# Attention's sums of later key blocks: added by VectorE before one product with the matrix of -1

## Chip, core and metric

The kernel runs on one core of a Trainium2 chip. The metric is the time of one execution on the device in microseconds (us); the number for a kernel is the median of its runs. The engines are called PE (TensorE), DVE (VectorE), ACT (ScalarE), POOL (GpSimd) and SP (SyncE, which issues the transfers here).

## What is computed

A trunk of two layers on 512 tokens of width 1024, in float32. Each layer is a SwiGLU feed-forward half, a token mixer and a second SwiGLU half, each between two RMSNorms. The change is in the mixer's attention: 8 heads of 64, strictly causal, with stick-breaking weights in place of a softmax. In the reference:

```python
z = jnp.einsum('bhqd,bhkd->bhqk', q_blk, kh).astype(jnp.float32) * scale
mask = k_pos[None, :] < q_pos[:, None]
log_keep = jnp.where(mask, jax.nn.log_sigmoid(-z), 0.0)
between = lax.cumsum(log_keep, axis=3, reverse=True) - log_keep
a = jnp.where(mask, jnp.exp(jax.nn.log_sigmoid(z) + between), 0.0)
return jnp.einsum('bhqk,bhkd->bhqd', a.astype(vh.dtype), vh)
```

Since log_sigmoid(-z) is -softplus(z), and log_sigmoid(z) is z - softplus(z), the exponent of a key is its z less the softplus of that key and of all later keys up to the query.

## The kernel before

Every matrix product is made of float32 values split in a high and a low part (the function `to_parts`, lines 507 to 513: a cast makes the high part, VectorE subtracts it from the value for the low part), so that TensorE multiplies several pairs of parts where plain arithmetic would have one product. Weights come from memory in units, one per tile `raw`, and are split by ScalarE (line 155, `wh`) and VectorE (line 156, `wl`). Weights and kept activations share a pool of `SLOTS` slots. The functions `load`, `split` and `ahead` (lines 140 to 172) keep a ledger of it: a unit is loaded if a slot is free beyond the reserved ones, and split if two are.

Attention works with keys on partitions and queries on columns, in key blocks of 128. A head (class `Head`) has three tiles in PSUM: tile 0 holds key block 2 (queries 256 to 511, its columns 0 to 255) and key block 3 (queries 384 to 511, columns 256 to 383), tile 1 holds key block 1 (queries 128 to 511, 384 columns), tile 2 key block 0 (512 columns).

`scores` computes z for each tile with the mask added on the diagonal blocks. Then ScalarE makes ln(1 + exp(-|z|)) in three instructions (lines 542 and 297), VectorE adds max(z, 0) (line 545), and `parts` splits the softplus: VectorE casts the high part pH (line 510) and subtracts for the low part pL (line 513).

`sums` then subtracts softplus values from z on TensorE, accumulating in the same PSUM tile. Within a key block this is a product with `ntri`, a triangle of -1. For the key blocks after it, it is a product with `none_`, a diagonal matrix of -1, which moves a softplus block of another tile onto these columns. Tile 1 needs the blocks 2 and 3 of tile 0, tile 2 needs those of tiles 1 and 0. Each such move is done for the high and for the low part. ScalarE then takes the exponential (line 297), which is split again (ScalarE casts at line 512, VectorE subtracts at line 513), and `values` multiplies it by v.

The instructions of TensorE stand in one fixed order (`mm` makes each follow the one before). Attention is a generator that the main line of the mixer's other projections polls between its products. After a head's scores come about 9.5 us of other products (`D_SUMS`, of which `values` of the previous head takes its share) and then its sums. The order on the other engines is the planner's: it takes what is ready, by program order. The softplus and attention parts of all heads take turns in `PB` pairs of buffers, other work tiles in `TB` = 7 buffers named t. Other work of VectorE during attention is splitting weights (line 156), the short convolution and the pooling (lines 664 to 701), queries and keys (lines 643 and 649), and the head's output (lines 590 and 513).

Of the kernel before, what the change touches and what calls it, by code (L numbers as in the profile page):

```python
# [12 lines left out]
ALU = mybir.AluOpType  # L13
PSUM = bass.MemoryType.PSUM

P = 128
T = 512
# [12 lines left out]
EPS = 1e-6  # L30
UNIT = KB * P
HEAD = 3
SLOTS = 28
RAW = 2
WARM = 24
URGENT = 0
# [1 line left out]
OUT_A = ((4, 6), (7,))  # L38
OUT_B = ((5, 0), (1, 2), (3,))
TB = 7  # L40
PB = 4
CB = 5

MASKED = -1e30
H_DVE = ('p0', 'p1', 'p2')

D_SUMS = 9.5
D_SCORES = 0.8
# [53 lines left out]
def trunk_kernel(ctx: ExitStack, tc: tile.TileContext, xt: bass.AP, wu: bass.AP,  # L102
                 consts: bass.AP, mats: bass.AP, gains: bass.AP, out: bass.AP):
    nc = tc.nc
# [10 lines left out]
    def uid(s):  # L115
        cnt[0] += 1
        return f"{s}_{cnt[0]}"
# [3 lines left out]

    slots = {"free": SLOTS, "reserve": CHUNKS[0]}

    def slot(name, dt=F32R):
        assert slots["free"] > 0, name
        slots["free"] -= 1
        return wpool.tile([P, 2, T], dt, tag="w", bufs=SLOTS, name=name)

# [71 lines left out]
    def tmp(shape=(P, T), dt=F32, tag="t", bufs=TB):  # L200
        return apool.tile(list(shape), dt, tag=tag, bufs=bufs, name=uid(tag))

    def bank(tag="d"):
        return ppool.tile([P, 512], F32, tag=tag, bufs=5 if tag == "z" else 3, name=uid("ps" + tag))
# [18 lines left out]
    def mm(dst, w, r, start, stop, us=None):  # L223
        ins = nc.tensor.matmul(dst, w, r, start=start, stop=stop, skip_group_check=True)  # L224
        if line["last"] is not None:
            after(ins, line["last"], "order")
        line["last"] = ins
        line["now"] += max(0.108, r.shape[-1] * 0.00042) if us is None else us
# [66 lines left out]
    def fn(out_, in_, f_, **kw):  # L295

        ins = nc.scalar.activation(out_, in_, f_, **kw)  # L297
        if last_load:
            after(ins, last_load[0], "activation table")
        last_fn[:] = [ins]  # L300
# [206 lines left out]
    def to_parts(dstH, dstL, src, what=None):  # L507

        if what in H_DVE:
            nc.vector.tensor_copy(dstH, src)  # L510
        else:
            nc.scalar.copy(dstH, src)  # L512
        nc.vector.tensor_tensor(dstL, src, f32(dstH), op=ALU.subtract)  # L513
# [5 lines left out]
    class Head:  # L519
# [6 lines left out]

        def scores(self):
            k, lh, q = (self.qk[n][:, self.e, :] for n in ("k", "lh", "q"))
            for ti, blocks in enumerate(TILES):
                z = bank("z")  # L530
                self.z.append(z)

                d, m = self.diagonals(z, blocks)
                mm(d, identr, m, True, True, 0.06 * len(blocks))
                for kb, col in blocks:
                    ks, qs = slice(kb * P, (kb + 1) * P), slice(kb * P, T)

                    for qq in (q, lh):
                        mm(z[:, col:col + T - kb * P], k[:, ks], qq[:, qs], False, True)
                n = WIDTH[ti]  # L540
                t = tmp()
                nc.scalar.activation(t[:, :n], z[:, :n], AF.Abs)  # L542
                fn(t[:, :n], t[:, :n], AF.Exp, scale=-1.0)
                fn(t[:, :n], t[:, :n], AF.Ln, bias=1.0)
                nc.vector.scalar_tensor_tensor(t[:, :n], z[:, :n], 0.0, t[:, :n],
                                               op0=ALU.max, op1=ALU.add)
                self.sp.append(self.parts(t, n, f"p{ti}"))

        def diagonals(self, t, blocks):

            n = len(blocks)
            d = t.rearrange("p (a b) -> p a b", b=P)[:, 0:2 * n - 1:2, :]
            return d, maskr.unsqueeze(1).to_broadcast((P, n, P))

        def parts(self, t, n, what):
            hi = tmp(dt=F32R, tag="pH", bufs=PB)
            lo = tmp(dt=F32R, tag="pL", bufs=PB)
            to_parts(hi[:, :n], lo[:, :n], t[:, :n], what)
            return hi, lo

        def sums(self):

            for ti, blocks in enumerate(TILES):
                z, n = self.z[ti], WIDTH[ti]
                for part in self.sp[ti]:
                    mm(z[:, :n], ntri, part[:, :n], False, True)

                for to, src, c0, w in (((P, 0, 256, P),), ((P, 0, 0, 256), (256, 0, 256, P)),
                                       ((P, 1, 0, 384), (256, 0, 0, 256), (384, 0, 256, P)))[ti]:
                    for part in self.sp[src]:  # L570
                        mm(z[:, to:to + w], none_, part[:, c0:c0 + w], False, True)
                t = tmp()
                fn(t[:, :n], z[:, :n], AF.Exp)
                self.a.append(self.parts(t, n, f"a{ti}"))
# [338 lines left out]
```

## Time and profile before

| what | value |
|---|---|
| time, median of 3 runs | 1927.26 us (1927.14 to 1928.81) |
| the profiled execution | 1925.21 us |
| its span, first to last instruction | 1923.4 us |
| instructions | 22094 |
| mean granted clock of TensorE | 0.992 of full speed |
| bytes read from memory, written | 176.65 MB, 2.10 MB |

All rows are of the one profiled execution, and their times count from the start of its span. In the page, each engine has its busy time, its share of the span and its count of instructions. A row of the timeline has the start, the duration (both us), engine, line, operation and tiles, and in brackets the idle time of the engine before it and who ended that. A row of the windows has the stretch and its length, then for PE, PEld (weight loads), DVE, ACT and POOL the busy time and the count of instructions, and then the granted clock of TensorE (1.00 is full speed), the share of the transfer engines and GB/s. A row of groups has line, engine, operation, tiles, shape and count, then busy us and mean ns of one, then the idle time before.

### The profile page before, as it was taken

To read this page: it belongs to the slowest core of one execution; us is meant where nothing else is said; L and a number is where in the kernel's file an instruction comes from. 1 tells how busy PE (TensorE), PEld (TensorE's weight loads), DVE (VectorE), ACT (ScalarE), POOL (GpSimd) and SP (SyncE) were. 2 spreads that over 40 slices of the span, in tenths; PEclk is the share of its full clock that TensorE was granted. 3 is DMA by queue.
4 is the path that set the end of the run, shared out by engine and by line. 5 is a ranking of instruction groups with operands and counts; after the bars stand their busy time and mean duration, and the time that the engine had idled before them with its cause. 6 is when DMAs were issued, how large, how long until landed. Compare 5 with 4: busy or idle time off the path is not lost.

```text
span 1923.4 us, 22094 instructions
## 1 busy us (share of the span) xinstructions
PE 1883.7 (98%) x9072; PEld 1587.3 (83%) x9072; DVE 876.2 (46%) x1154; ACT 719.7 (37%) x1137; POOL 47.6 (2%) x68
## 2 busy tenths in 40 slices
PE   7999999999999999999999999999999999999998
PEld 5888888888878988888898888888888788888887
DVE  5323333567767422333463223336577663223333
ACT  4323222357764323222242222224477542322221
POOL 1000000000001000000010000000000010000000
PEclk8999999999999999999999999999999999999999
DMA  5213233131023223223142222422111242222311
GB/s 207 99 67 131 77 111 108 44 131 55 34 75 144 88 77 120 77 99 121 55 143 88 99 87 88 142 77 99 66 55 44 88 140 91 99 88 88 132 66 44
DMA packets 50645, 180.17 MB, mean 94 GB/s; under 512 B 5744, under 2 KB 5872, under 8 KB 50544
## 3 DMA queue, kind: packets, MB, share of 16 engines
q1 hardware_dynamic: 50544, 178.76, 27.0%
q8 instruction: 71, 1.16, 0.2%
q14 instruction: 30, 0.25, 0.0%
HBM read 176.65 MB, written 2.10 MB: 93 GB/s over the span
## 4 chain that ended last, share of the span: by engine, by line
PE 91%; DVE 4%; ACT 2%; issue 1%; DMA 1%; POOL 0%; SPq 0%; DVEq 0%; POOLq 0%; ACTq 0%
PE psz L224 80%; PE psd L224 11%; DVE wl L156 1%; PE psd L266 1%; DVE f L322 0%; DMA raw<-in_w_dram 0%; ACT t L297 0%; DVE f L362 0%; DVE hl L335 0%; DMA g<-in_gains_dram 0%; DVE x L376 0%; DVE pL L513 0%; POOL ss L313 0%; ACT pH L512 0%; ACT t L542 0%
## 5 line engine op out<-in xcount | busy, mean ns | idle before, releaser
L224 PE MATMUL psz<-hl,wh 128*128 128x512 f32 (+1 forms) x1536 | 566.3, 369 | 6.4 <-DVE hl L335 6.4
L224 PE MATMUL psz<-hh,wh 128*128 128x512 f32 (+1 forms) x1536 | 566.7, 369 | 4.3 <-ACT hh L334 4.3
L224 PE MATMUL psz<-hh,wl 128*128 128x512 f32 (+1 forms) x1536 | 565.5, 368 | 0.0
L156 DVE TENSOR_TENSOR wl<-raw,wh 128x1024 fp32r<-128x1024 f32 x324 | 387.0, 1211 | 313.4 <-ACT wh L155 244.2
L224 PE MATMUL psz<-wh,hid 128*128 128x512 f32 x1408 | 437.1, 390 | 0.0
L155 ACT CAST wh<-raw 128x1024 fp32r<-128x1024 f32 x324 | 328.5, 1038 | 223.4 <-PE psz L224 180.3
L224 PEld LDWEIGHTS psz<-hl,wh 128*128 128x128 f32 x1536 | 291.8, 190 | 54.6 <-DVE hl L335 7.4
L224 PEld LDWEIGHTS psz<-hh,wh 128*128 128x128 f32 x1536 | 291.7, 190 | 52.6 <-ACT hh L334 5.3
L224 PEld LDWEIGHTS psz<-hh,wl 128*128 128x128 f32 x1536 | 291.7, 190 | 47.4
L224 PEld LDWEIGHTS psz<-wh,hid 128*128 128x128 f32 x1408 | 264.3, 188 | 54.7
L224 PE MATMUL psz<-wl,hid 128*128 128x512 f32 x704 | 273.9, 389 | 0.0
L448 DVE TENSOR_TENSOR t<-t,psz 128x512 f32<-128x512 f32 x84 | 57.7, 687 | 470.3 <-PE psz L224 470.3
L449 ACT CAST hid<-t 128x512 fp32r<-128x512 f32 x88 | 54.6, 620 | 450.4 <-DVE t L448 450.4
L297 ACT ACTIVATE t<-psz 128x512 f32<-128x512 f32 (+1 forms) x136 | 77.5, 573 | 227.5 <-PE psz L224 226.6
L224 PEld LDWEIGHTS psz<-wl,hid 128*128 128x128 f32 x704 | 132.2, 188 | 27.2
L224 PE MATMUL psd<-hh,wh 128*128 128x512 f32 (+1 forms) x320 | 119.7, 374 | 0.0
L224 PE MATMUL psd<-hh,wl 128*128 128x512 f32 (+1 forms) x320 | 118.0, 369 | 0.0
L224 PE MATMUL psd<-hl,wh 128*128 128x512 f32 (+1 forms) x320 | 118.0, 369 | 0.0
L450 DVE TENSOR_TENSOR hid<-t,hid 128x512 fp32r<-128x512 f32 x88 | 61.0, 693 | 60.8 <-ACT hid L449 60.8
L313 POOL TENSOR_TENSOR ss<-ss,expo 128x1 f32<-128x1 f32 x48 | 39.1, 815 | 1689.7 <-DVE ss L372 1586.1
L224 PEld LDWEIGHTS psd<-hh,wl 128*128 128x128 f32 x320 | 60.3, 189 | 10.3
L224 PEld LDWEIGHTS psd<-hl,wh 128*128 128x128 f32 x320 | 60.4, 189 | 10.1 <-issue 0.5
(98 smaller groups left out, 1437.4 us busy)
## 6 DMA issues: line engine op xcount, KB each, us to landing
raw<-in_w_dram SPq DMA_DIRECT2D x316, 512.0 KB, 3.3
g<-in_gains_dram SPq DMA_DIRECT2D x12, 512.0 KB, 5.0
x<-in_xt_dram SPq DMA_DIRECT2D x4, 512.0 KB, 8.7
raw<-in_w_dram SPq DMA_DIRECT2D x8, 256.0 KB, 2.7
out_dram<-x SPq DMA_DIRECT2D x8, 256.0 KB, 2.1
mat<-in_mats_dram SPq DMA_DIRECT2D x1, 384.0 KB, 9.4
mat<-in_mats_dram SPq DMA_DIRECT2D x1, 64.0 KB, 3.2
cst<-in_consts_dram SPq DMA_DIRECT2D x1, 25.0 KB, 9.2
```

The lines of the kernel that those rows point to most:

```text
L155: nc.scalar.copy(h[:, :n], raw[:, :n])
L156: nc.vector.tensor_tensor(lo[:, :n], raw[:, :n], f32(h[:, :n]), op=ALU.subtract)
L224: ins = nc.tensor.matmul(dst, w, r, start=start, stop=stop, skip_group_check=True)
L266: ins = nc.tensor.transpose(dst, src, ident)
L297: ins = nc.scalar.activation(out_, in_, f_, **kw)
L313: nc.gpsimd.tensor_tensor(r, ms, expo, op=ALU.pow)
L448: nc.vector.tensor_tensor(u, g, pu, op=ALU.mult)
L449: nc.scalar.copy(t[:, 0, :], u)
L450: nc.vector.tensor_tensor(t[:, 1, :], u, f32(t[:, 0, :]), op=ALU.subtract)
```

## The change

Three additions on VectorE, as soon as tile 1's softplus is there, make one tile s of 512 columns: its columns 256 to 511 hold, for the queries 256 to 511, the softplus of blocks 2 and 3 added together, and its columns 0 to 255 hold that plus the softplus of block 1 for the same queries. This tile is split in parts once, with the high part cast by VectorE (`'later'` in `H_DVE`). The sums of tile 1 then move 256 columns of it with `none_`, and those of tile 2 move 256 columns of it, and 128 of tile 1's own. The part buffers grow from four pairs to five, and a slot is taken from the pool of weights.

```diff
-SLOTS = 28
+SLOTS = 27
-PB = 4
+PB = 5
-H_DVE = ('p0', 'p1', 'p2')
+H_DVE = ('p0', 'p1', 'p2', 'later')
...
         def scores(self):
             k, lh, q = (self.qk[n][:, self.e, :] for n in ("k", "lh", "q"))
+            ts = []
             for ti, blocks in enumerate(TILES):
...
                 self.sp.append(self.parts(t, n, f"p{ti}"))
+                ts.append(t)
+                if ti == 1:
+
+                    s = tmp()
+                    nc.vector.tensor_copy(s[:, 256:384], ts[0][:, :P])
+                    nc.vector.tensor_tensor(s[:, 384:], ts[0][:, P:256], ts[0][:, 256:384], op=ALU.add)
+                    nc.vector.tensor_tensor(s[:, :256], s[:, 256:], t[:, P:384], op=ALU.add)
+                    self.later = self.parts(s, T, "later")
...
-                for to, src, c0, w in (((P, 0, 256, P),), ((P, 0, 0, 256), (256, 0, 256, P)),
-                                       ((P, 1, 0, 384), (256, 0, 0, 256), (384, 0, 256, P)))[ti]:
-                    for part in self.sp[src]:
+                for to, src, c0, w in (((P, self.sp[0], 256, P),), ((P, self.later, 256, 256),),
+                                       ((P, self.sp[1], 0, P), (256, self.later, 0, 256)))[ti]:
+                    for part in src:
                         mm(z[:, to:to + w], none_, part[:, c0:c0 + w], False, True)
```

## Rows read from the trace of the kernel before

**Rows 1.** The page, busy time of each engine.

```profile
PE 1883.7 (98%) x9072; PEld 1587.3 (83%) x9072; DVE 876.2 (46%) x1154; ACT 719.7 (37%) x1137; POOL 47.6 (2%) x68
```

**Rows 2.** Waits of TensorE: us in total, times, longest us.

```profile
PE psz L224 <- DVE pL L513: 6.0, 10, 1.1
```

**Rows 3.** Windows: heads 0 and 1 of layer 0, then two stretches after head 6.

```profile
434.29:442.88 8.59, 8.59 (x44) 7.34 (x43) 6.97 (x14) 2.76 (x6) 0.00 (x0) 1.00 0.19 61
447.79:454.56 6.77, 6.77 (x37) 5.94 (x36) 6.73 (x13) 5.26 (x9) 0.00 (x0) 1.00 0.08 32
...
545.00:548.40 3.40, 3.40 (x16) 3.40 (x16) 2.31 (x5) 1.71 (x5) 0.00 (x0) 0.50 0.05 17
1493.00:1496.40 3.40, 3.40 (x23) 3.10 (x23) 2.98 (x5) 2.68 (x7) 0.00 (x0) 1.00 0.03 10
```

**Rows 4.** Timeline of VectorE: last pL of heads 0, 1, 4, 5, 7.

```profile
437.95 0.69 DVE L513 TENSOR_TENSOR pL<-t,pH 128x512 fp32r<-128x512 f32 x1
...
451.47 1.15 DVE L513 TENSOR_TENSOR pL<-t,pH 128x384 fp32r<-128x384 f32 x2
...
506.86 0.69 DVE L513 TENSOR_TENSOR pL<-t,pH 128x512 fp32r<-128x512 f32 x1
...
517.56 0.69 DVE L513 TENSOR_TENSOR pL<-t,pH 128x512 fp32r<-128x512 f32 x1
...
555.76 1.15 DVE L513 TENSOR_TENSOR pL<-t,pH 128x384 fp32r<-128x384 f32 x2
```

**Rows 5.** Timeline of TensorE: ntri by pL, heads 2 to 7.

```profile
472.64 0.45 PE L224 MATMUL psz<-pL,ntri 128*128 128x384 f32 x1 [0.27 <-DVE pL L513]
...
485.95 0.44 PE L224 MATMUL psz<-pL,ntri 128*128 128x384 f32 x1 [0.69 <-DVE pL L513]
...
508.39 0.39 PE L224 MATMUL psz<-pL,ntri 128*128 128x512 f32 x1
...
520.08 0.39 PE L224 MATMUL psz<-pL,ntri 128*128 128x512 f32 x1
...
542.61 0.45 PE L224 MATMUL psz<-pL,ntri 128*128 128x384 f32 x1 [1.10 <-DVE pL L513]
...
544.47 0.50 PE L224 MATMUL psz<-pL,ntri 128*128 128x512 f32 x1 [0.73 <-DVE pL L513]
...
557.86 0.39 PE L224 MATMUL psz<-pL,ntri 128*128 128x512 f32 x1
```

**Rows 6.** Timeline of TensorE, products with the matrix of -1, tile 2.

```profile
473.85 0.34 PE L224 MATMUL psz<-pH,none__73 128*128 128x384 f32 x1
474.02 0.34 PE L224 MATMUL psz<-pL,none__73 128*128 128x384 f32 x1
...
474.43 0.22 PE L224 MATMUL psz<-pH,none__73 128*128 128x128 f32 x1
474.49 0.27 PE L224 MATMUL psz<-pL,none__73 128*128 128x128 f32 x1
```

**Rows 7.** Groups by shape on VectorE: busy us, mean ns, idle before.

```profile
L513 DVE TENSOR_TENSOR pL<-t,pH 128x384 fp32r<-128x384 f32 x64 | 34.9, 553 | 6.3 <-ACT pH L512 6.0
...
L513 DVE TENSOR_TENSOR pL<-t,pH 128x512 fp32r<-128x512 f32 x32 | 22.0, 688 | 11.0 <-ACT pH L512 10.6
...
L510 DVE CAST pH<-t 128x512 fp32r<-128x512 f32 x16 | 6.7, 418 | 0.0
...
L823 DVE CAST ntri<-mat 128x128 fp32r<-128x128 f32 x1 | 0.2, 224 | 0.0
```

**Rows 8.** Groups on VectorE within head 6's window, 534.83 to 544.47.

```profile
L156 DVE TENSOR_TENSOR wl<-raw,wh 128x1024 fp32r<-128x1024 f32 (+1 forms) x3 | 3.1, 1043 | 0.0
```

**Rows 9.** Timeline: splits of the last value weights, then TensorE's first use.

```profile
388.01 1.22 DVE L156 TENSOR_TENSOR wl<-raw,wh 128x1024 fp32r<-128x1024 f32 x1
...
390.88 1.22 DVE L156 TENSOR_TENSOR wl<-raw,wh 128x1024 fp32r<-128x1024 f32 x1
...
396.27 0.39 PE L224 MATMUL psz<-wh,hh 128*128 128x512 f32 x1
```

## The prediction

> **What bounds the kernel now.** I read the page's busy shares first: TensorE (PE) is busy nearly all of the span, VectorE (DVE) less than half of it [rows 1]. So time taken off TensorE is time off the span, wherever it stays fed. The list of what TensorE waits for comes next: the waits inside the program's attention are waits for pL, the low part that VectorE writes [rows 2]. They are 6.0 us in ten pieces, which is small, but they say that in places VectorE is already the engine that sets the end of attention's sums.
>
> That is why VectorE's 46% must not be read as room. It is a mean over the feed-forward layers, where VectorE idles, and attention. So I read the windows that matter: one for each head, from VectorE's first softplus instruction (line 545) to the moment when TensorE starts the last product of that head that needs a softplus (ntri by pL, 512 columns). Head 0's window of 8.59 us leaves VectorE 1.62 idle, head 1's of 6.77 only 0.04 [rows 3]. From head 1 on it is full exactly where the change puts work.
>
> Full is not late, since some of what VectorE does in a window is not urgent (weights split for later, convolution, pooling). Lateness is read from the end of the head's last pL on VectorE against the start of its product on TensorE [rows 4, 5]: head 1, 451.47 + 1.15 = 452.62 against 454.56, the end of its window [rows 3], 1.94 us to spare; head 4, 507.55 against 508.39, 0.84; head 5, 518.25 against 520.08, 1.83; head 7, 556.91 against 557.86, 0.95. Head 0, with no head before it, ends at 437.95 + 0.69 = 438.64 against 442.88, the end of its window: 4.24, more than the change can take. Heads 2, 3 and 6 have less than nothing: TensorE stands 0.27, 0.69 and 1.10 + 0.73 us for them [rows 5]. These are 2.8 of the 3.0 us that [rows 2] leave for a layer; layer 1 repeats layer 0.
>
> **What goes, part by part.** Counted from the code, for each head and each of the two parts (high, low), the matrix of -1 multiplied 128 columns for tile 0, 256 + 128 for tile 1, 384 + 256 + 128 for tile 2. After the change it is 128, 256, 128 + 256. So one product of 384 and one of 128 columns go, twice: 4 of 12 matmuls. What they cost is the distance between starts, not the duration, because matmuls overlap: a 384 takes 474.02 - 473.85 = 0.17 us, a 128 takes 474.49 - 474.43 = 0.06 us [rows 6]. Per head 2 x (0.17 + 0.06) = 0.46 us; 16 heads: 7.4 us, 0.38% of the time. This is the most that the removal itself can give.
>
> Each of these matmuls also loads the matrix of -1 anew, and the start distance of 0.06 us shows that the load is hidden. [...]
>
> **What comes.** Five VectorE instructions a head: a copy of 128 columns, an add of 128, an add of 256, then the split of the 512 columns into a cast and a subtraction. The last two are on show: 0.42 and 0.69 us [rows 7]. An add of two SBUF operands goes by the subtraction's rows: (688 - 553) / 128 = 1.05 ns a column, so 0.28 us for 128 and 0.42 for 256. A float copy of 128 columns isn't in the trace; the cast of 128 took 224 ns, the bounds are nothing and the 0.28 of an add, I take 0.22. Sum 2.03 us of durations. Neighbours in VectorE's queue overlap by about 0.1 us where independent, so what they displace lies between 1.6 and 2.0; I take 1.9. Over 16 heads that is 30 us more for an engine with 1047 us idle overall, and nearly none idle in these windows.
>
> **When it is due.** TensorE comes to the end of the sums sooner, by the two lost 128s of tile 1, 0.1 us. And the sum's low part is needed before tile 2's, about half a microsecond earlier than the instant against which I measured (one product of the sum's 256 columns and the 512-column ntri product of the high part stand between). So each head must find 1.9 + 0.3 = 2.2 us (1.7 at least, 2.6 at most). If VectorE keeps its order and puts off nothing, the new stall of a head is 2.2 less its spare time: heads 0 to 7: 0, 0.3, 2.2, 2.2, 1.4, 0.4, 2.2, 1.3 = 10.0 us a layer, 20 in both. The same sum with 1.7 and 2.6 gives 6.7 and 12.6 a layer.
>
> Against it: VectorE's order isn't fixed by hand; the planner places what is ready, by program order. The five instructions stand in the program ahead of the weight splits and the pooling that fill the same windows, so some of this will go behind them, and splitting weights later costs nothing where they lie ready early. But it can't all go: the chain copy, add, add, cast, subtraction is serial, and in the gaps between its links a ready split of about 1 us slips in, as three do in head 6's window today, 3.1 us [rows 8].
>
> **The remaining edits.** One weight slot less (28 to 27) moves some splits one place later in the ledger of slots. The tightest place that I found is the last weight of the value projection in a mixer: its split starts 2.9 us after the one before it (390.88, 388.01) and ends at 392.10; TensorE first needs it at 396.27 [rows 9]. One place later it would end at about 395.0: hidden, with 1.3 us left. I charge nothing; a second place would cost 2.9 - 1.3 = 1.6 us a mixer. A fifth pair of part buffers is there because a head now makes seven pairs for six. The second tile's pair no longer has to wait for the previous head's values, the sum's does instead. At best this ring also ends the present waits, at worst it changes nothing; I charge nothing. The longer life of tile 0's t costs nothing as long as 7 buffers serve 8 uses a head; no row shows a wait for t.
>
> **The rivals.** *All is put off* (other sign): VectorE moves enough pooling and weight splitting behind the chain that no stall is added. In head 6's window there are 3.1 us of splits alone [rows 8], more than its 2.2. Then the full 7.4 us is kept: 1919.9. It decides if less than 3.7 us a layer of new stalls remains. *Nothing is put off*: 20 - 7.4 = +12.6, 1939.9; bounds 6.7 and 12.6 a layer give 1933.3 to 1945.1. *The ring helps*: besides the full saving the 6.0 us of waits in [rows 2] go: -13.4, 1913.9. *Weights come late*: +1.6 a mixer or more on top of half the stalls, 1934. *The clock.* After head 6's stalls in layer 0, the granted clock was 0.50 from 545.0 to 548.4, and TensorE began 16 matmuls in the time in which layer 1, after the same stalls, began 23 at 1.00 [rows 3]: half of 3.4 us lost, 1.7 us, sometimes. More stalls mean more such stretches; I charge one. [...]
>
> **How the numbers follow.** Likeliest: half of the 20 us is put off. Then -7.4 + 10.0 + 1.7 = +4.3 against the profiled execution's 1925.2, which is itself 2.0 below the median of the runs; against the median the 1.7 may be there already in part, so I take +3.7: 1931 us. Chances: half put off 0.33 (nearly as often within 0.2% as above it, seldom below), all put off 0.28 (nearly always faster), nothing put off 0.25, weights late 0.08, ring helps 0.06. A difference of 0.2% (3.9 us) is about what a measurement of this kernel can tell from no change. Faster: 0.25 + 0.06 + 0.03 = 0.34; slower: 0.25 + 0.13 + 0.03 = 0.41; the same: 0.25. Range: from all of the saving, 1919.5, to nothing put off at its middle price, 1940; the ring and the dear half of "nothing" are left out. The likeliest case's own range is 1927 to 1935.
>
> **What would show it.** 64 matmuls with the matrix of -1 a layer instead of 96, at the same start distances: if not, the first step is wrong. TensorE's waits for what VectorE writes at lines 510 and 513: some 10 us more than the 6.0 of [rows 2] is the forecast; about 6.0 again is "all put off", 26 is "nothing". If the weight splits of line 156 and the pooling's instructions have left the head windows, VectorE reordered. New waits of TensorE on wl would be the slot. A clock of 0.5 at 471 to 490 or 540 to 550 would be stalls charged twice. I'm wrong if new stalls are under 3.7 us a layer or lie elsewhere.

## The result: slower by 1.07%, and where the time went

| what | before | after |
|---|---|---|
| time, median | 1927.20 us (4 runs) | 1946.56 us (4 runs, 1945.43 to 1947.10) |
| ratio, with its 95% interval | | 1.0107 (1.0095 to 1.0118) |
| span of the profiled execution | 1923.4 us | 1944.6 us |
| mean granted clock of TensorE | 0.992 | 0.986 |

The forecast was 1931 us, the range 1919.5 to 1940: slower was the likeliest sign, but the size lies outside.

The profile after is read in the order of the prediction. First the page's busy times, which answer to [rows 1]:

```profile
PE 1888.2 (97%) x9008; PEld 1586.9 (82%) x9008; DVE 901.2 (46%) x1234; ACT 725.2 (37%) x1137; POOL 55.7 (3%) x68
```

64 matmuls are gone and 80 instructions of VectorE have come, as counted. VectorE's share is still 46%: the number that had to be distrusted has not moved. VectorE's busy time rose by 901.2 - 876.2 = 25.0 us, 1.56 a head. What TensorE waits for is the list that answers to [rows 2]:

```profile
PE psz L224 <- DVE pL L513: 20.4, 18, 2.2
PE psd L266 <- DVE f L325: 10.3, 2, 7.7
PE psd L266 <- DVE ss L372: 7.5, 3, 2.8
PE psz L224 <- DVE hl L335: 6.6, 3, 2.6
PE psz L224 <- ACT pH L512: 1.6, 2, 0.8
PE psz L224 <- DVE pH L510: 1.2, 2, 0.6
...
```

In the kernel before, these rows stand beside the one of [rows 2]:

```profile
PE psd L266 <- DVE f L325: 11.1, 4, 8.3
PE psz L224 <- DVE hl L335: 6.4, 4, 2.6
...
PE psz L224 <- ACT hh L334: 4.3, 2, 2.4
...
PE psz L224 <- DVE pH L510: 0.9, 2, 0.5
...
```

The waits for what VectorE writes at lines 510 and 513 were 0.9 + 6.0 = 6.9 us and are 1.2 + 20.4 = 21.6. A wait by way of line 372, at layer boundaries, is new, and the one on line 334 is gone. The whole list sums to 32.9 us before and 49.3 after: 16.4 us more of an idle TensorE.

The rest is clock. These windows answer to the last two of [rows 3]: two stretches that follow long waits, one after that, and one in layer 1 (columns as before; the third column from the right is the granted clock; read in windows of 0.1 us over the whole span it is 1.00 in 18908 of 19445 and 0.50 in 520, and between them in 17, at the changes):

```profile
492.20:495.60 3.40, 3.40 (x11) 2.80 (x10) 2.44 (x6) 2.58 (x5) 0.00 (x0) 0.50 0.47 151
...
553.60:560.40 6.80, 5.86 (x20) 5.15 (x20) 3.61 (x8) 4.03 (x10) 0.00 (x0) 0.50 0.02 4
560.50:567.30 6.80, 6.80 (x34) 5.71 (x33) 6.80 (x15) 4.00 (x7) 0.00 (x0) 1.00 0.00 1
1447.90:1454.70 6.80, 6.22 (x17) 5.07 (x18) 5.03 (x8) 4.91 (x8) 0.00 (x0) 0.50 0.23 78
```

In 6.8 us at 0.50 TensorE begins 20 matmuls (0.94 us of it is a wait), in the next 6.8 us 34. Over the span, (1 - 0.986) x 1944.6 = 27.2 us of clock are lost, against (1 - 0.992) x 1923.4 = 15.4: 11.8 us more, uncertain by some 2 us because the clock is given to three digits. Now the account of the two profiled executions closes: -7.4 for the products, +16.4 of waits, +11.8 of clock are +20.8 us; the spans differ by 21.2. TensorE's busy time agrees: it rose by 1888.2 - 1883.7 = 4.5 us, where -7.4 + 11.8 is 4.4.

By place, the stretches at half clock inside attention explain it. In the kernel before there is one, of 3.4 us (after head 6 of layer 0, [rows 3]). In the changed kernel there are five: 3.4 us after head 3 and 6.8 us at head 6 in layer 0, then 6.8, 3.4 and 6.8 us at heads 3, 4 and 6 in layer 1. That is 27.2 us for 3.4, so 13.6 us lost for 1.7. None follows heads 1, 2 and 5, with waits of 0.7 to 1.2 us each, nor head 4 of layer 0, which waits as long (1.55 us) as head 4 of layer 1 (1.56). Outside of attention, the layer boundaries lose 3.4 us both before (one stretch of 6.8 us at 606) and after (two of 3.4 us, at 400 and 1356).

Head 6 shows how a wait comes about. VectorE's timeline, from the third of the new instructions (line 555) to the sum's low part, with the starts that count:

```profile
545.49 0.42 DVE L555 TENSOR_TENSOR t<-t,t 128x256 f32<-128x256 f32 x1
...
547.35 0.41 DVE L510 CAST pH<-t 128x512 fp32r<-128x512 f32 x1
547.68 1.21 DVE L156 TENSOR_TENSOR wl<-raw,wh 128x1024 fp32r<-128x1024 f32 x1
548.82 0.74 DVE L678 SCALAR_TENSOR_TENSOR c<-c,cst,c 128x511 f32<-128x511 f32 x1
549.48 0.68 DVE L546 SCALAR_TENSOR_TENSOR t<-psz,t 128x512 f32<-128x512 f32 x1
550.19 0.69 DVE L599 TENSOR_TENSOR t<-psz,t 64x512 f32<-64x512 f32 x1
550.91 0.69 DVE L156 TENSOR_TENSOR wl<-raw,wh 128x512 fp32r<-128x512 f32 x1
551.52 0.68 DVE L513 TENSOR_TENSOR pL<-t,pH 128x512 fp32r<-128x512 f32 x1
```

And TensorE's, in the same stretch, which answers to the rows of head 6 in [rows 5]:

```profile
549.21 0.22 PE L224 MATMUL psz<-pH,none__73 128*128 128x128 f32 x1
549.27 0.28 PE L224 MATMUL psz<-pL,none__73 128*128 128x128 f32 x1
549.38 0.39 PE L224 MATMUL psz<-pH,ntri 128*128 128x384 f32 x1
...
552.26 0.38 PE L224 MATMUL psz<-pL,none__73 128*128 128x256 f32 x1 [2.20 <-DVE pL L513]
553.26 0.51 PE L224 MATMUL psz<-pH,ntri 128*128 128x512 f32 x1 [0.61 <-DVE pH L510]
554.70 0.80 PE L224 MATMUL psz<-pL,ntri 128*128 128x512 f32 x1 [0.94 <-DVE pL L513]
```

The sum is there at 545.9 and its high part at 547.8, but its low part comes at 552.2: weight splits, a step of the convolution, tile 2's own softplus (line 546) and an earlier head's output stand between. TensorE waits 2.20, 0.61 and 0.94 us, 3.75 in all where it was 1.83, and at 553.6 the clock falls. The window of [rows 8] has grown from 9.64 to 12.09 us (542.61 to 554.70). It holds two weight splits, of 1024 and of 512 columns, where [rows 8] has three; but the third of those starts at 544.33, 0.14 us before the window's end, so that only two stood ahead of the sums in the kernel before as well. In this head no split was put off behind them.

### The profile page after: what moved, and what is told of

Its sections match the earlier page's. It is cut to its first block, busy times and chain, and to the rows that moved or that the text cites. A ratio compares the mean times of both kernels' runs of the same rounds, so it can differ in the third digit from the quotient of the medians.

```text
span 1944.6 us, 22070 instructions
## 1 busy us (share of the span) xinstructions
PE 1888.2 (97%) x9008; PEld 1586.9 (82%) x9008; DVE 901.2 (46%) x1234; ACT 725.2 (37%) x1137; POOL 55.7 (3%) x68
## 4 chain that ended last, share of the span: by engine, by line
PE 85%; DVE 9%; ACT 3%; issue 2%; POOL 1%; DMA 1%; SPq 0%; DVEq 0%; POOLq 0%; ACTq 0%
PE psz L224 76%; PE psd L224 8%; DVE wl L156 1%; DVE pL L513 1%; ACT t L297 1%; POOL ss L313 1%; DVE t L546 1%; DVE pH L510 1%; DMA raw<-in_w_dram 1%; PE psd L266 1%; DVE f L322 1%; DVE f L362 1%; DVE x L376 1%; ACT t L543 0%; DVE t L599 0%
## 5 line engine op out<-in xcount | busy, mean ns | idle before, releaser
L224 PEld LDWEIGHTS psz<-wl,hid 128*128 128x128 f32 x704 | 132.3, 188 | 27.2
L313 POOL TENSOR_TENSOR ss<-ss,expo 128x1 f32<-128x1 f32 x48 | 47.0, 978 | 1681.6 <-DVE ss L372 1570.4
L513 DVE TENSOR_TENSOR pL<-t,pH 128x384 fp32r<-128x384 f32 (+1 forms) x112 | 66.8, 608 | 21.2 <-ACT pH L512 18.7
L224 PEld LDWEIGHTS psd<-hh,wh 128*128 128x128 f32 x320 | 62.2, 194 | 10.6 <-PE psd L224 0.5
```

What stands on the lines that cost most here:

```text
L313: nc.gpsimd.tensor_tensor(r, ms, expo, op=ALU.pow)
```

## The experiments

The waits below are those of TensorE for the pL and pH that VectorE writes at lines 510 and 513, from each run's own profile. Each ratio is to the kernel before on the same chip, whose medians there were 1926.15 us (e1 to e4), 1925.02 (e5 to e8) and 1924.81 (e9 to e12).

| run | slots, pairs, D_SUMS | ratio (95% interval) | median us | waits us | clock |
|---|---|---|---|---|---|
| before | 28, 4, 9.5 | 1 | | 6.9 | 0.992 |
| after | 27, 5, 9.5 | 1.0107 (1.0095 to 1.0118) | 1946.56 | 21.6 | 0.986 |
| e1_slot | 27, 4, 9.5 | 1.0012 (1.0003 to 1.0021) | 1928.35 | 6.8 | 0.992 |
| e2_ring | 27, 5, 9.5 | 1.0011 (1.0002 to 1.0020) | 1927.85 | 6.8 | 0.992 |
| e3_cut | 28, 4, 9.5 | 0.9977 (0.9968 to 0.9986) | 1920.52 | 8.0 | 0.991 |
| e4_four | 28, 4, 9.5 | 1.0118 (1.0105 to 1.0132) | 1948.72 | 23.8 | 0.984 |
| e5_last | 27, 5, 9.5 | 1.0139 (1.0124 to 1.0154) | 1951.89 | 26.3 | 0.984 |
| e6_own | 27, 4, 9.5 | 1.0122 (1.0105 to 1.0139) | 1948.25 | 21.2 | 0.986 |
| e7_late | 27, 5, 12.5 | 0.9976 (0.9967 to 0.9986) | 1920.65 | 4.3 | 0.991 |
| e8_cost | 27, 5, 9.5 | 1.0135 (1.0120 to 1.0150) | 1950.34 | 19.3 | 0.986 |
| e9_before_late | 28, 4, 12.5 | 0.9956 (0.9944 to 0.9969) | 1917.83 | 0.4 | 0.993 |
| e10_late_28 | 28, 4, 12.5 | 0.9927 (0.9915 to 0.9939) | 1910.70 | 4.2 | 0.993 |
| e11_narrow | 28, 4, 12.5 | 0.9930 (0.9917 to 0.9944) | 1910.75 | 1.7 | 0.993 |
| e12_mid | 27, 5, 11.0 | 1.0044 (1.0031 to 1.0056) | 1933.14 | 11.9 | 0.986 |

**e1_slot: the lost slot alone.** The kernel before with:

```diff
-SLOTS = 28
+SLOTS = 27
```

> The kernel before with one weight slot less (27 for 28) and nothing else. Theory 1 (the slot makes the new waits at the layer boundaries, the additions make those in attention): TensorE gets the three waits on VectorE line 372 that the changed kernel shows at 399, 989 and 1355 us (2.3, 2.8 and 2.4 us), saves about 3.7 us of its waits at 606 and 1552, and has one or two more stretches at half clock, 1.7 us each; in all +2 to +6 us, 1929 to 1933; its waits on pL in attention stay near 6. Theory 2 (the waits at the boundaries too come from the planner's order around the new instructions): within 2 us of the kernel before, no wait on line 372.

Measured: +0.12%, 2.2 us by the medians. The three waits by way of line 372 are there (7.1 us, against none before), and in return the wait on line 334 (4.3 us) is gone and that on line 325 is 9.2 us for 11.1. So the boundary waits belong to the slot, as theory 1 says, though they cost less than the 1929 to 1933 us expected.

**e2_ring: slot and ring of buffers, without the arithmetic.** In addition to e1_slot:

```diff
-PB = 4
+PB = 5
```

> The kernel before with 27 slots and five pairs of part buffers, without the additions: all of the change but its arithmetic. Theory 1: the same time as with the slot alone, within 2 us, and waits on pL in attention of 4 to 7 us. Theory 3 (the ring of buffers changes VectorE's order, and that makes the new waits in attention): the waits on pL rise towards 20 us, and the time to 1940 and more.

Measured: the same as e1_slot, with waits in attention unchanged at 6.8 us. Theory 3 falls for this order of the work: the ring by itself changes nothing.

**e3_cut: the saving alone.** The kernel before with:

```diff
-                for to, src, c0, w in (((P, 0, 256, P),), ((P, 0, 0, 256), (256, 0, 256, P)),
-                                       ((P, 1, 0, 384), (256, 0, 0, 256), (384, 0, 256, P)))[ti]:
+                for to, src, c0, w in (((P, 0, 256, P),), ((P, 0, 0, 256),),
+                                       ((P, 1, 0, P), (256, 0, 0, 256)))[ti]:
```

> The kernel before with the four matmuls of a head cut and no additions on VectorE; left out are the softplus sums of the blocks beyond the nearest ones. It measures the saving by itself. Theory 1: 7.4 us less on TensorE, waits as before (6 to 7 us), so 1919.5 to 1921. Theory 4 (TensorE only comes sooner to waits that end at the same time, since VectorE's chain sets them): waits on pL rise by about 1 us or more and the gain is 5 us or less.

Measured: -0.23% (-0.14 to -0.32), 4.4 us by the ratio and 5.6 by the medians. It is a gain, but less than 7.4: the waits on lines 510 and 513 rose from 6.9 to 8.0 us, and all the waits together from 32.9 to 34.9. About a quarter of what TensorE saves here it spends waiting, as theory 4 has it, though the median alone would also fit theory 1.

**e4_four: the change without the lost slot and without the fifth pair.** The changed kernel with `SLOTS = 28` and `PB = 4`.

> The changed kernel with 28 slots and four pairs of part buffers for its seven pairs a head. Theory 1: no wait on line 372 at the boundaries, the waits in attention stay near 20 us, time about 1938 to 1942. Theory 3: with four pairs the sum's and the next two pairs must wait for the values of the head before, the waits in attention rise to 25 us or more, and the time is 1945 or more.

Measured: 1.0118, no better than the change (the intervals overlap). The waits by way of line 372 are gone, but attention's are 23.8 us and the clock is 0.984. Giving the slot back does not make the change fast, which agrees with the 0.12% of e1_slot. Of the two expectations neither is met in full: the time is theory 3's, the waits lie between. Two edits were made at once, so what four pairs cost here may hide what the slot gives.

**e5_last: the same instructions, in another place.** The additions and the split of their sum stand after the loop over the tiles:

```diff
-                if ti == 1:
-                    s = tmp()
...
-                    self.later = self.parts(s, T, "later")
+            s = tmp()
...
+            self.later = self.parts(s, T, "later")
```

> The changed kernel with the three additions and the split of their sum written behind tile 2's softplus in the program instead of before it; the same instructions. Theory A (VectorE simply has 2 us more to do before the sums end): the waits on lines 510 and 513 stay within 3 us of the 21.6 of the changed kernel, time within 3 us of 1946.6. Theory B (the place of the new tile delays tile 2: in the changed kernel ScalarE's first instruction on tile 2 comes after four others of the softplus instead of after one fewer tile's worth, and its pair is made last): ScalarE takes tile 2 early again as before, the waits fall to 15 us or less, time 1940 or less.

Measured: 1.0139, waits 26.3 us. ScalarE does take tile 2 early again (its first instruction on head 6's tile 2 starts 1.30 us after that on tile 0, against 2.55 in the changed kernel), but the waits did not fall; now the sum's low part is what comes last. Theory B falls: the order decides which part is late, not whether one is. Theory A's bounds are passed too, by 1.7 us of waits and 2.3 us of time: this order is the worse one.

**e6_own: the sum outside of the ring of t.**

```diff
-PB = 5
+PB = 4
...
-                    s = tmp()
+                    s = tmp(tag="s", bufs=2)
```

> The changed kernel with the sum in two buffers of its own instead of the seven of the tiles t, paid for by the fifth pair of part buffers (four pairs, as in the run with four pairs and 28 slots; here 27). Theory A: waits in attention as in that run, 22 to 26 us, time 1948 to 1951. Theory B, if it is the turn in the ring of t that holds tile 2 back: ScalarE takes tile 2 early, waits 17 us or less, time 1943 or less.

Measured: 1.0122 and 21.2 us of waits, just under theory A's 22 to 26, and far from theory B's 17. ScalarE does take tile 2 early here (at head 6, 1.31 us after tile 0, as in the kernel before; e4_four, which has four pairs too, has 2.55), so the turn of the t buffers does hold tile 2 back in the changed kernel; but it is not the cause of the waits.

**e7_late: the same work, given 3 us more.** The changed kernel with:

```diff
-D_SUMS = 9.5
+D_SUMS = 12.5
```

> The changed kernel with 12.5 us in place of 9.5 of other products between a head's scores and its sums, so that VectorE has 3 us more; same work. Theory A and B both: nearly all waits in attention end before TensorE comes, 5 us or less remain, the half-clock stretches in attention go, and 14 us of waits and 10 us of clock come back: 1920 to 1926, unless the last head then has too little other work behind it (then waits of up to 3 us a layer at the end of attention, 1926 to 1932). Rival (TensorE's fixed order is not the point; VectorE falls behind for good and carries its delay from head to head): waits of 15 us and more stay.

Measured: 0.9976, waits 4.3 us, and no stretch at half clock in attention (mean clock 0.991 for 0.986). The same instructions now run 1.3% faster than in the changed kernel, and faster than the kernel before. This speaks for lateness: VectorE does all of the added work, and the loss is gone when TensorE comes later. (The planner orders VectorE anew for each kernel, so that an effect of its order is not wholly excluded.) What is left against the control with the same number (e9_before_late) is 0.2%, and e10_late_28 takes that back. VectorE does not carry a delay from head to head, so the rival falls.

**e8_cost: the additions without the saving.** The changed kernel with the loop of the sums of before:

```diff
-                for to, src, c0, w in (((P, self.sp[0], 256, P),), ((P, self.later, 256, 256),),
-                                       ((P, self.sp[1], 0, P), (256, self.later, 0, 256)))[ti]:
-                    for part in src:
+                for to, src, c0, w in (((P, 0, 256, P),), ((P, 0, 0, 256), (256, 0, 256, P)),
+                                       ((P, 1, 0, 384), (256, 0, 0, 256), (384, 0, 256, P)))[ti]:
+                    for part in self.sp[src]:
```

> The changed kernel with its additions and the split of the sum, but with the twelve products of before on TensorE; the sum is computed and not used. It measures the cost alone, by the side of the run that cut the matmuls alone. If cost and saving add up: 1946.6 + 5.6 to 7.4 = 1952 to 1954. If waiting for the sum itself is what costs (TensorE does not need it here): waits in attention 12 us or less and time 1940 or less.

Measured: 1.0135, waits 19.3 us. Cost and saving very nearly add up: 1.35% - 0.23% is 1.12%, and the change has 1.07%. TensorE needn't even wait for the sum: VectorE's own lateness with the softplus parts makes nearly all of it.

**e9_before_late: the control.** The kernel before with `D_SUMS = 12.5`.

> The kernel before with 12.5 us for 9.5 between scores and sums: the control for the run of the changed kernel with 12.5. Theory A: its waits on lines 510 and 513 (6.9 us) go and with them a half-clock stretch, so -3 to -9 us, 1917 to 1923, and the changed kernel's gain over this one is then only what is left of the saved products. Rival (12.5 costs something by itself, at the end of attention or by heads that take longer to start): no gain or a loss, 1925 to 1930.

Measured: 0.9956, waits 0.4 us. The kernel before was late in its own sums as well, and more time alone is worth 7 us to it. Of the gain of e7_late this much is not the change's: at the same 12.5 us the change with 27 slots and five pairs is some 0.2% slower, with intervals that just overlap, and not faster.

**e10_late_28: the change with time, and with the slot.** The changed kernel with `D_SUMS = 12.5`, `SLOTS = 28`, `PB = 4`.

> The changed kernel with 12.5, and with 28 slots and four pairs of part buffers. Theory A, and the slot's price of 2 us: waits of 5 to 8 us in attention, no waits on line 372, 1916 to 1921, some 2 us under the run with 12.5 and 27 slots. Rival (with four pairs and later sums the head's pairs wait for each other): 1922 or more, waits above 10 us.

Measured: 0.9927 (0.9915 to 0.9939), 1910.70 us: faster than both kernels, and than the control, whose interval does not touch this one. It is also less than the 1916 to 1921 expected. By the medians it is 7.1 us under the control. The profiled executions show less, 1912.3 - 1908.6 = 3.7 us, and tell why, in the control first and then here:

```profile
PE 1880.5 (98%) x9072; PEld 1586.2 (83%) x9072; DVE 876.8 (46%) x1154; ACT 717.7 (38%) x1137; POOL 47.6 (2%) x68
```

```profile
PE 1872.8 (98%) x9008; PEld 1577.4 (83%) x9008; DVE 900.0 (47%) x1234; ACT 719.6 (38%) x1137; POOL 47.6 (2%) x68
```

At the same clock, 0.993, TensorE is busy 7.7 us less: this is what the removed products are worth. Its waits are 28.9 us against 24.9, of which 4.2 against 0.4 are on lines 510 and 513, and take 4.0 of it back. The rest of the 7.1 goes with the clock: two of the control's five runs have 0.993 (1913.6 and 1914.1 us) and three 0.990 to 0.991 (1917.8 to 1919.0), and the median is one of the latter; all five of this kernel have 0.993. Why the control's clock falls more often is open. This kernel is also 9.9 us under e7_late by the medians, far more than the slot's 2.2 in e1_slot. The profiled spans differ by 12.3 us, of which the waits account for 36.1 - 28.9 = 7.2 (the waits by way of line 372 among them, 7.8 us against none), and TensorE's busy time, at a clock of 0.991 against 0.993, for 5.0. Whether the slot or the fifth pair does this was not tried apart.

**e11_narrow: less work where nothing is late.** As e10_late_28, with no copy and a sum of 384 columns; tile 1's product with 256 columns of the sum becomes two with 128:

```diff
-                    nc.vector.tensor_copy(s[:, 256:384], ts[0][:, :P])
-                    nc.vector.tensor_tensor(s[:, 384:], ts[0][:, P:256], ts[0][:, 256:384], op=ALU.add)
-                    nc.vector.tensor_tensor(s[:, :256], s[:, 256:], t[:, P:384], op=ALU.add)
-                    self.later = self.parts(s, T, "later")
+                    nc.vector.tensor_tensor(s[:, 256:384], ts[0][:, P:256], ts[0][:, 256:384], op=ALU.add)
+                    nc.vector.tensor_tensor(s[:, :P], ts[0][:, :P], t[:, P:256], op=ALU.add)
+                    nc.vector.tensor_tensor(s[:, P:256], s[:, 256:384], t[:, 256:384], op=ALU.add)
+                    self.later = self.parts(s, 384, "later")
...
-                for to, src, c0, w in (((P, self.sp[0], 256, P),), ((P, self.later, 256, 256),),
+                for to, src, c0, w in (((P, self.sp[0], 256, P),), ((P, self.sp[0], 0, P), (256, self.later, 256, P)),
```

> As the run before this one, with a sum of 384 columns for 512: the copy is gone, tile 1 takes blocks 2 from its own parts, and VectorE has about 0.35 us less a head. Theory A: little is left to gain where TensorE comes late, so within 2 us of it, waits at most 2 us fewer. If VectorE's work still sets the end: 3 us or more less.

Measured: 0.9930, the same as e10_late_28, with waits of 1.7 us for 4.2. The time is as theory A says, but the run does not show that less work for VectorE is worth nothing. TensorE has 32 products more (9040 for 9008): all its waits are 4.6 us less (24.3 for 28.9) and its busy time 4.5 us more (1877.3 for 1872.8), and the two cancel.

**e12_mid: half of the time.** The changed kernel with `D_SUMS = 11.0`.

> The changed kernel with 11.0 for 9.5. Theory A in numbers: each head's wait falls by about 1.5 us down to nothing, so of some 21.6 us on lines 510 and 513 some 6 to 9 stay, with two or three half-clock stretches in attention instead of seven: 1925 to 1932, between the two. If the waits come from the order rather than from the time that VectorE has: no such fall, 1938 or more.

Measured: 1.0044, waits 11.9 us, clock 0.986. It lies between the two as expected, but higher: nearly half of the waits went, and the clock over the span did not rise. Eight stretches at half clock begin between head 3 of the first attention (489 us) and the end of the second layer's mixer (1562 us). Five of them are in attention, with at least 17.9 us at 0.50, where the changed kernel has five with 27.2 us and I had reckoned with two or three; three are at layer boundaries.

## Why the prediction was wrong

**The step that failed** is the one on the clock: "More stalls mean more such stretches; I charge one", 1.7 us. The clock lost 11.8 us more than before. It was a term with a row behind it, and the row itself warned: after 1.10 + 0.73 us of waits the clock fell in one layer and not in the other [rows 3]. The term took one stretch for both layers; the changed kernel has five in attention, three of them twice as long, after heads 3, 4 and 6. Of the 16.9 us by which the spans' difference of 21.2 passes the forecast's sum of 4.3, the clock is 10.1 and the waits 6.4. The case "nothing is put off" had no clock in it at all, which is why its 1940 bounded the range. That a longer wait lowers the clock is read from which heads are followed by such a stretch (in the changed kernel those with 1.56 to 3.75 us of waits, none with 1.55 us or less); no run changed the waits alone, and e12_mid has 9.7 us less of them at the same mean clock.

**The stalls** were mis-sized second. I took half of 20 us, 10; they rose by 21.6 - 6.9 = 14.7. The sum by heads was near in all (waits added in layer 0: heads 1 to 7: 1.2, 0.8, 1.2, 1.6, 0.9, 1.9, 0, together 7.6, for 10.0 forecast at full price), but the discount was not: I argued that the planner would put other work behind the new chain. In the two heads looked at it did not. In head 6 both splits ahead of the sums stayed there, and in head 1 a split came in front of tile 2's low part, which in the kernel before had run first. The three splits of [rows 8], from which the case "all is put off" took its 3.1 us, were a misreading: the third is all but outside of the window, and 1.9 us were there to put off. That the total stayed under 20 is due to heads 2, 3 and 7, which lost less than I reckoned. The price was too high as well: VectorE's busy time rose by 1.56 us a head, under the 1.6 to 2.0 of the forecast. The forecast's own sum with 1.56 + 0.3 in place of 2.2, and nothing put off, gives 15.1 us for both layers; since its heads fit less well (nothing for head 1, 1.9 for heads 2 and 3), that it comes so near to 14.7 is in part luck.

**The slot** I charged at nothing, and it is +0.12% by itself (e1_slot). I looked for it in late weights; no wait of TensorE on wl came. It works at the layer boundaries, through the order of VectorE's work, as told below.

**What held.** The prices: the copy of 128 columns took 220 ns, the adds 284 and 418, against 0.22, 0.28 and 0.42 us; the cast 414 and the subtraction 685. These are the groups of the changed kernel that answer to [rows 7]:

```profile
L513 DVE TENSOR_TENSOR pL<-t,pH 128x512 fp32r<-128x512 f32 x48 | 32.6, 685 | 15.2 <-ACT pH L512 14.9
L510 DVE CAST pH<-t 128x512 fp32r<-128x512 f32 x32 | 13.2, 414 | 0.0
...
L555 DVE TENSOR_TENSOR t<-t,t 128x256 f32<-128x256 f32 x16 | 6.7, 418 | 0.0
L554 DVE TENSOR_TENSOR t<-t 128x128 f32<-128x128 f32 x16 | 4.5, 284 | 0.0
L553 DVE COPY t<-t 128x128 f32<-128x128 f32 x16 | 3.5, 220 | 0.0
```

The saving held too: TensorE's busy time is 7.7 us less in e10_late_28 than in its control, for 7.4 forecast. But its working was not right. The low part's product of 128 columns does start 0.06 us after the high part's (549.21 and 549.27 above), as in [rows 6], yet the product behind it starts only 0.11 us later (549.38). So a pair of 128 takes 0.17 us, not 0.12, and the sum becomes 16 x (0.34 + 0.17) = 8.2 us. The 0.06 us show the weight load, which takes 0.19 us there, hidden behind the first product of a pair only; what makes the next step 0.11 us was not shown. The ring as a cost of nothing held without the additions (e2_ring). And so did the main reading, that VectorE is full where the work was put, and late: the same work given 3 us more takes the kernel from 1.07% over the one before to 0.24% and 0.73% under it (e7_late, e10_late_28), of which 0.44% come from the 3 us alone (e9_before_late).

## What to carry to other kernels

An engine at 46% of the span can be the one that ends a stage; before work is moved onto it, find the windows in which another engine waits for it, and count the spare time there, instruction by instruction. If the spare time is short, move the moment at which the result is needed, together with the work: the same change is at +1.07% or -0.24% here by one number in the schedule. Then give the old kernel the same number before crediting the change: alone it is worth 0.44%. And where TensorE's clock has been seen to fall after a wait, price further waits with a stretch at half clock too, as a range; in attention the clock cost 11.9 us here beside 14.7 us of waits.

## What had not been expected of the hardware

GpSimd took 2.60 us for an instruction that takes it 0.55 elsewhere. The inverse root of the norm (line 313) takes it 0.55 us in 33 of its 48 executions in the kernel before. In e1_slot, before the third set of transposes, it takes 2.60, by the timeline of VectorE and POOL:

```profile
395.91 1.21 DVE L156 TENSOR_TENSOR wl<-raw,wh 128x1024 fp32r<-128x1024 f32 x1
...
396.13 2.60 POOL L313 TENSOR_TENSOR ss<-ss,expo 128x1 f32<-128x1 f32 x1 [8.45 <-DVE ss L323]
...
397.05 1.28 DVE L366 TENSOR_TENSOR t<-f,g 128x512 f32<-128x512 f32 x2
...
398.77 0.75 DVE L325 TENSOR_SCALAR f<-f,ss 128x1024 f32<-128x1024 f32 x1 [0.44 <-POOL ss L313]
...
399.74 0.55 POOL L313 TENSOR_TENSOR ss<-ss,expo 128x1 f32<-128x1 f32 x1 [1.00 <-DVE ss L372]
```

A root of one value a partition ends here at 398.73, 0.40 us after the end of VectorE's run of three instructions (a weight split, then two products with the gain) at 398.33; with VectorE idle beside it, at 399.74, it takes 0.55. It is not so each time: the root at 976.30 in the same execution takes 1.40 us and ends while a product with the gain is running. In the kernel before, 15 roots start while an instruction of lines 156, 322 or 366 runs on VectorE; they take 0.92 to 2.60 us, and each ends 0.40 to 0.41 us after that instruction or the unbroken run of such. The other 33 take 0.55, ten of them with line 335 running beside them. In e1_slot 2.05 us are added to an instruction of 0.55; what adds them was not tried by an experiment of its own.

This slow root is only a small part of the slot's boundary wait. TensorE's transposes wait 2.39 us there, and VectorE stands idle 0.44 us for the root. Over the whole execution VectorE waits 7.9 us for roots before line 325, against 7.2 in the kernel before. The larger part is that VectorE comes late to this norm: line 323 starts at 395.84, against 392.01 in the kernel before. A weight split stands ahead of line 376 in e1_slot (387.57 and 389.31), where line 376 was first before (386.68, the split at 388.01). Why one slot less leads to that order was not followed further.
